# Relative biases and stores of keys and values on GpSimd's queue in a two-layer encoder step

## The chip, the cores and the metric

The kernel runs on one core of one Trainium2 chip. Its metric is device time in microseconds (us). Before the change the median is 974.71 us, of three runs of 974.71, 974.99 and 973.73 us. The engines are TensorE (PE: matmuls; PEld: its weight loads), VectorE (DVE), ScalarE (ACT), GpSimd (POOL) and SyncE (SP). SP computes nothing here: it issues DMA transfers, in the order of its own queue.

## The reference, cut to what matters

One inference step of an encoder of two layers, with 256 prompt tokens and 32 sample tokens, 1024 features, 16 heads of 64 features, all in fp32:

```
layer 0:  q,k,v of 8 heads "A" and 8 heads "B" = rmsnorm(x) @ w_in_ab
          A: s = q k^T / 8 + rel_bias[clip(pos_q - pos_k, -128, 128)]    # per head
             a query sees its own 64-token chunk and the 8 chunks before it; o = softmax(s) v
          B: stick-breaking attention (strictly causal, no softmax, no bias)
          x += [oA, oB] @ w_out_ab
layer 1:  q,k,v of 16 heads, lf = log_sigmoid(z + b_f);  c = cumsum(lf)
          s = q k^T / 8 + c_q - c_k, causal;  o = softmax(s) v;  x += o @ w_out_c
each layer then: cross-attention of 4 heads into 256 memory tokens
                 (mk, mv = rmsnorm(memory) @ w_xk, w_xv), and a SwiGLU feed-forward
returned: y, the k and v of every layer and head, lf, mk and mv of both layers
```

The sample tokens attend to cached keys and values of 128 past tokens, and to themselves. In layer 0 a prompt query thus adds to its scores, for each head, a row of the relative-distance table that starts one place later for each query; in layer 1 the bias is made from cumulative sums. Keys, values and memory keys and values are results as well as operands, so each is stored to DRAM.

## The kernel before

Features lie on the 128 partitions and the 288 tokens (256 prompt, 32 sample) along the free axis. Every fp32 product is made of three matmuls of split operands, high times high, high times low, low times high (L68 is the one line for all matmuls).

**Weights** come in units of 1024x128 (512 KB). `unit` loads one through SP (L136) into one of four buffers `st`; ACT copies it to a rounded high half `hi` (L141, five buffers), DVE subtracts to get the low half `lo` (L142, four buffers). `split_scaled` makes `hh` and `hl` (L248) of the normalized inputs in the same way, and `split` makes `kh`, `kl` and `vh`, `vl` (L314, L315) of memory keys and values; `kl` and `vl` are subtracted on POOL. POOL also adds up squares for norms (`ssq`, L213).

**Head pairs.** In both layers `pairs` runs j = 0 to 7 over pairs of heads. For each, `proj(j)` projects q, k and v (three units); `evac_kv` writes k or v to a buffer `kv` and stores it at once (L728). Then `attend(j)` starts a generator, every second pair a generator for the sample tokens, and `memory.steps` projects a few blocks of memory keys (`mk`, stored as `mkT`, L551) and values (`mv`, stored, L571) into the stream of the projections. The generators advance by a step at each `tick`, which every projection calls, so that softmax work of one pair runs beside the matmuls of the next projections.

**Softmax.** For each head the scores `sc` go to `softmax`: DVE adds the bias and takes the row maximum in one instruction (L348, one for each of the two query tiles, which have 128 and 256 key columns), ACT takes the exponential with a row sum (L350), DVE the reciprocal (L351), and DVE multiplies (L353). Then PE transposes `e` (L372 to L374). The sample's tile is `es`, transposed at L399.

**Biases in layer 0.** `rel_lines` loads the table (L737), DVE fills its left part (L738, `line`), and it is stored to DRAM (L740, `lined`). Eight copies from DRAM to DRAM (L743, one for each head) write it 128 times with rows of 385, `skew`, from which any window reads as a matrix whose rows are shifted by one. `rel_prompt` reads a head's two windows into a tile `bi` (L753: 128 columns for the first query tile, L754: 256 for the second) and POOL masks two 64x64 corners (L755, L756). Both windows are windows of the same matrix: the first tile's 128 columns are the second's columns 128 to 255. `rel_sample` makes four small loads into `bs` (L762).

**Biases in layer 1.** `gate` stores the cumulative sums (L856 `cumd`, L863 `cumsd`); `attend` loads them across partitions (L894, `ck`), and POOL subtracts and masks (L899 to L902, `bc`). For the sample, SP loads `bcs` and `cq`, and POOL subtracts and masks at L918 and L921.

**Order.** Instructions are put in order on each engine by the framework's scheduler, and each engine runs its own queue in that order; an instruction whose operand isn't ready holds up all that stand behind it on that engine. All DMA transfers of this kernel are issued by SP, so a store that waits for its data holds up the loads behind it in the same way.

## Time and profile before

| | before |
|---|---|
| median of the runs | 974.71 us (973.73 to 974.99) |
| profiled execution, own time | 973.61 us |
| its span, granted clock of TensorE | 971.8 us, 0.995 |
| PE busy | 951.7 us (98% of the span) |
| DVE, ACT, POOL busy | 588.5, 483.6, 195.9 us (61%, 50%, 20%) |
| moved by DMA | 163.59 MB, 168 GB/s in the mean |
| stores of keys and values `kv` | 32, of 144 KB each |
| stores `mkT`, `mv` | 16 and 16, of 128 KB each |
| copies `skew` | 8, of 192 KB each |
| bias loads `bi` | 8 of 128 KB and 8 of 64 KB |

How to read rows of it. A row of the timeline is: start in us from the span's beginning, duration in us, engine, source line, operation, output<-input, partitions x elements, type, and how often it runs in a row; in square brackets the idle time of that engine just ahead of it, and what ended it. SPq and POOLq are those engines' issues of DMA transfers. A row of the waits is engine and line, what it waited for, us in total, how often, and the longest. A row of the groups is line, engine, operation, output<-input, count | busy us, mean ns of one | idle time before it, and what ended most of it. A row on DMA issues gives count, KB each, and the median us from issue to landing.

### The profile page before, as it was taken

The page shows a single profiled execution, that of the slowest core. Times are in us where ns is not written, and L with a number is a line of the kernel's source. Part 1 is how long each engine was busy: PE and PEld are TensorE (multiplying, and loading weights), DVE is VectorE, ACT ScalarE, POOL GpSimd, SP SyncE. Part 2 cuts the span into 40 slices and gives each one's busy share as a digit, 9 for nine tenths or more (in the row PEclk, how much of TensorE's full clock was granted, in tenths as well). Part 3 has the DMA queues.
Part 4 walks back from the last instruction along what each step waited for, and adds up shares of the span by engine and source line. Part 5 has one row for each costly group of instructions (what it writes and reads, how often), then busy time and mean ns, then how long its engine had stood idle before and what let it go on. Part 6 is the DMA issues. An engine that isn't in the chain of part 4 may idle for free.

```text
span 971.8 us, 19089 instructions
## 1 busy us (share of the span) xinstructions
PE 951.7 (98%) x7477; PEld 919.4 (95%) x7477; DVE 588.5 (61%) x1135; ACT 483.6 (50%) x854; POOL 195.9 (20%) x293
## 2 busy tenths in 40 slices
PE   8999999999999999999999999999999999999995
PEld 7889999999999999999998999999989999999995
DVE  6687555676765555854565666657757655555452
ACT  4556868554554444443445555545546544444330
POOL 3111002210213222411004324213002222222010
PEclk9999999999999999999999999999999999999998
DMA  7775455544354444554465455545425444454431
GB/s 232 253 250 186 140 182 175 177 157 152 104 168 166 160 174 161 187 196 164 162 209 174 168 201 174 185 162 185 158 86 174 153 173 165 161 174 168 159 108 49
DMA packets 60137, 163.59 MB, mean 168 GB/s; under 512 B 8160, under 2 KB 21520, under 8 KB 60048
## 3 DMA queue, kind: packets, MB, share of 16 engines
q1 hardware_dynamic: 60048, 162.38, 49.7%
q8 instruction: 59, 0.97, 0.4%
q14 instruction: 30, 0.25, 0.1%
HBM read 152.20 MB, written 11.72 MB: 169 GB/s over the span
## 4 chain that ended last, share of the span: by engine, by line
PE 91%; DVE 3%; DMA 2%; issue 1%; ACT 1%; SPq 0%; POOL 0%; DVEq 0%; ACTq 0%; POOLq 0%
PE pj L68 51%; PE dn L68 14%; PE op L68 11%; PE mv L68 5%; DMA st<-w_ab 1%; PE xo L68 1%; PE po L68 1%; PE xs L68 1%; PE zb L68 1%; DVE lo L142 1%; PE sc L68 1%; PE nr L68 1%; PE nrm L68 1%; PE xss L68 1%; DMA x<-xT 0%
## 5 line engine op out<-in xcount | busy, mean ns | idle before, releaser
L141 ACT CAST hi<-st 128x1024 fp32r<-128x1024 f32 x260 | 272.6, 1051 | 333.3 <-issue 146.0
L68 PE MATMUL pj<-hh,hi 128*128 128x288 f32 (+1 forms) x1352 | 405.3, 300 | 0.0
L68 PE MATMUL pj<-hl,hi 128*128 128x288 f32 (+1 forms) x1352 | 398.6, 295 | 1.7 <-DVE hl L248 1.7
L68 PE MATMUL pj<-hh,lo 128*128 128x288 f32 (+1 forms) x1352 | 399.2, 295 | 0.0
L142 DVE TENSOR_TENSOR lo<-st,hi 128x1024 fp32r<-128x1024 f32 x260 | 322.8, 1242 | 125.3 <-PE dn L68 41.2
L68 PEld LDWEIGHTS pj<-hh,hi 128*128 128x128 f32 x1352 | 255.8, 189 | 6.0 <-issue 4.2
L68 PEld LDWEIGHTS pj<-hl,hi 128*128 128x128 f32 x1352 | 256.0, 189 | 3.3 <-DVE hl L248 3.2
L68 PEld LDWEIGHTS pj<-hh,lo 128*128 128x128 f32 x1352 | 255.7, 189 | 0.0
L68 PE MATMUL dn<-fh,hi 128*128 128x288 f32 x400 | 108.5, 294 | 0.0
L68 PE MATMUL dn<-fh,lo 128*128 128x288 f32 x352 | 103.3, 294 | 0.0
L68 PE MATMUL dn<-fl,hi 128*128 128x288 f32 x304 | 89.5, 294 | 0.0
L68 PE MATMUL op<-ol,hi 128*128 128x288 f32 x256 | 75.8, 297 | 0.0
L68 PE MATMUL op<-oh,hi 128*128 128x288 f32 x256 | 75.5, 297 | 0.0
L68 PE MATMUL op<-oh,lo 128*128 128x288 f32 x256 | 75.2, 294 | 0.0
L68 PEld LDWEIGHTS dn<-fh,hi 128*128 128x128 f32 x400 | 72.3, 188 | 0.0
L68 PEld LDWEIGHTS dn<-fh,lo 128*128 128x128 f32 x352 | 66.2, 188 | 0.0
L213 POOL TENSOR_TENSOR ssq<-ssq,sq 128x288 f32<-128x288 f32 (+1 forms) x37 | 35.6, 963 | 120.3 <-ACT sq L202 78.3
L68 PEld LDWEIGHTS dn<-fl,hi 128*128 128x128 f32 x304 | 57.1, 188 | 0.0
L693 POOL TENSOR_TENSOR fl<-us,fh 128x288 fp32r<-128x288 f32 x38 | 32.9, 865 | 119.3 <-ACT fh L692 119.3
L688 DVE TENSOR_TENSOR us<-pj,rstd 128x288 f32<-128x288 f32 x44 | 20.1, 457 | 59.9 <-PE pj L68 59.9
L689 POOL TENSOR_TENSOR gs<-gs,sg 128x288 f32<-128x288 f32 x44 | 38.9, 883 | 76.1 <-ACT sg L687 76.1
L68 PEld LDWEIGHTS op<-ol,hi 128*128 128x128 f32 x256 | 48.2, 188 | 0.6 <-issue 0.4
(253 smaller groups left out, 1202.7 us busy)
## 6 DMA issues: line engine op xcount, KB each, us to landing
st<-w_gate SPq DMA_DIRECT2D x44, 512.0 KB, 3.3
st<-w_up SPq DMA_DIRECT2D x44, 512.0 KB, 3.2
st<-w_down SPq DMA_DIRECT2D x44, 512.0 KB, 3.2
st<-w_c SPq DMA_DIRECT2D x25, 512.0 KB, 3.3
st<-w_ab SPq DMA_DIRECT2D x23, 512.0 KB, 4.3
st<-w_xk SPq DMA_DIRECT2D x16, 512.0 KB, 3.5
st<-w_xv SPq DMA_DIRECT2D x16, 512.0 KB, 3.4
st<-w_xq SPq DMA_DIRECT2D x16, 512.0 KB, 4.2
```

The lines of the kernel that those rows point to most:

```text
L68: T.matmul(out, lhsT, rhs, start=start, stop=stop, skip_group_check=True)
L141: S.copy(hi[:, b], st[:, b])
L142: V.tensor_tensor(lo[:, b], st[:, b], hi[:, b].bitcast(F32), ALU.subtract)
L213: eng.tensor_tensor(s[:, :self.n], self.acc[i][:, :self.n], q[:, :self.n], ALU.add)
L688: V.tensor_tensor(us, pu[:, :NT], cur.r, ALU.mult)
L689: G.tensor_tensor(gs, gs, sg, ALU.mult)
L693: G.tensor_tensor(lo, us, hi.bitcast(F32), ALU.subtract)
```

## The change

A name `SIDE` for GpSimd is added, and these transfers are issued by it and no longer by SP: the load and store of the bias line, the eight skew copies, the bias loads of layer 0 for prompt and sample, and all stores of `kv`, `mkT` and `mv`. Loads of weights, of the caches and of `ck`, `bcs` and `cq`, and the stores of `lf`, `cumd`, `cumsd` and the result, stay with SP. In `rel_prompt` one load of 256 columns takes the place of two loads of 128 and 256, and one memset of the masked corner the place of two; `softmax` gets a start column of the bias for each query tile (`at`: 128 and 0), since both tiles now read the same 256 columns. Names and arithmetic are otherwise as they were; lines after L43 move down by one or two (L348 is L350 now, L740 is L742, L743 is L745).

```diff
     V, S, G, T, DMA = nc.vector, nc.scalar, nc.gpsimd, nc.tensor, nc.sync
+    SIDE = nc.gpsimd
...
-    def softmax(s, cols, bias, out):
+    def softmax(s, cols, bias, out, at=None):
...
-                V.tensor_tensor_reduce(out=out[:, c0:c1], in0=s[:, c0:c1], in1=bias[:, c0:c1], scale=-1.0, scalar=3e38,
+                b0 = at[i] if at else c0
+                V.tensor_tensor_reduce(out=out[:, c0:c1], in0=s[:, c0:c1], in1=bias[:, b0:b0 + c1 - c0], scale=-1.0, scalar=3e38,
...
-                DMA.dma_start(a["mkT"][l, i], t[:, 0:NP])
+                SIDE.dma_start(a["mkT"][l, i], t[:, 0:NP])
...
-                        DMA.dma_start(a["mv"][l, t, :, hd * 256:hd * 256 + 256], v[:, 0:NP])
+                        SIDE.dma_start(a["mv"][l, t, :, hd * 256:hd * 256 + 256], v[:, 0:NP])
...
             V.tensor_tensor(t, p[:, :NT], cur.r, ALU.mult)
-            DMA.dma_start(dst, t)
+            SIDE.dma_start(dst, t)
...
-        DMA.dma_start(ln[:, 128:384], a["rel"][:, 0:256])
+        SIDE.dma_start(ln[:, 128:384], a["rel"][:, 0:256])
...
-        DMA.dma_start(d, ln)
+        SIDE.dma_start(d, ln)
...
-            DMA.dma_start(bass.AP(tensor=sk.tensor, ...
+            SIDE.dma_start(bass.AP(tensor=sk.tensor, ...
...
-        DMA.dma_start(t[:, 0:128], rel_rows(sk, h, 256, P, 128))
-        DMA.dma_start(t[:, 128:384], rel_rows(sk, h, 128, P, 256))
-        G.memset(t[0:64, 64:128], NEG)
-        G.memset(t[0:64, 320:384], NEG)
+        SIDE.dma_start(t[:, 0:256], rel_rows(sk, h, 128, P, 256))
+        G.memset(t[0:64, 192:256], NEG)
...
-            DMA.dma_start(t[32 * h:32 * h + 32, 0:160], rel_rows(sk, 4 * g + h, 128, NS, 160))
+            SIDE.dma_start(t[32 * h:32 * h + 32, 0:160], rel_rows(sk, 4 * g + h, 128, NS, 160))
...
-                return attend_prompt(..., o[0][j], o[1][j])
+                return attend_prompt(..., o[0][j], o[1][j], (128, 0))
```

The scheduler makes another order from it on DVE, ACT, POOL and SP; the order on PE stays. Three places are shown, numbers behind the names of tiles counting them.

**The first bias of layer 0.** SP before, from the line's store to the loads of pair 0 and the weights behind them:

```order
L740 DMA lined<-line 8x384
L136 DMA st_398<-w_ab 128x1024
L136 DMA st_462<-w_ab 128x1024
L743 DMA skew<-lined 128x384 x8
L753 DMA bi_388<-skew 128x128
L754 DMA bi_388<-skew 128x256
L753 DMA bi_393<-skew 128x128
L754 DMA bi_393<-skew 128x256
L136 DMA st_508<-w_ab 128x1024
```

POOL in the changed kernel, the same piece of work:

```order
L742 DMA lined<-line 8x384
L745 DMA skew<-lined 128x384 x8
L756 DMA bi_388<-skew 128x256
L756 DMA bi_391<-skew 128x256
L756 DMA bi_545<-skew 128x256
L756 DMA bi_548<-skew 128x256
L763 DMA bs_555<-skew 32x160
L757 MEMSET bi_388 64x64
L763 DMA bs_555<-skew 32x160
L757 MEMSET bi_391 64x64
```

Pair 0 has the tiles `bi_388` and `bi_391` (before `bi_393`), pair 1 `bi_545` and `bi_548`. POOL now issues the loads for pair 1 and one for the sample ahead of the first mask. On DVE the line's copy, which the store waits for, stands elsewhere; before:

```order
L98 CAST ntrir<-ntri 128x128
L248 SCALAR_TENSOR_TENSOR hl_197<-x_81,gain,hh_196 128x288
L738 COPY line<-line 8x128
L248 SCALAR_TENSOR_TENSOR hl_201<-x_82,gain,hh_200 128x288
```

and in the changed kernel:

```order
L249 SCALAR_TENSOR_TENSOR hl_205<-x_82,gain,hh_204 128x288
L143 TENSOR_TENSOR lo_295<-st_292,hi_294 128x1024
L125 TENSOR_SCALAR ident<-warm 128x128
L214 TENSOR_TENSOR ssq_226<-sq_222,sq_224 128x288
L128 TENSOR_TENSOR fold<-ident 128x64
L740 COPY line<-line 8x128
L143 TENSOR_TENSOR lo_348<-st_345,hi_347 128x1024
```

The copy moved behind the splits of all of the input and of a weight unit.

**The softmax of pair 1 in layer 0, on DVE.** Before, from the second head's bias (`bi_554`) to the normalized rows:

```order
L348 ISA e_629,st_630<-sc_626,bi_554 128x256
L348 ISA st_630 128x1
L351 RECIPROCAL st_618<-st_618 128x2
L348 ISA es_647,st_648<-ss_638,bs_563 128x160
L348 ISA st_648 128x1
L353 TENSOR_SCALAR e_617<-e_617,st_618 128x128
L353 TENSOR_SCALAR e_617<-e_617,st_618 128x256
L142 TENSOR_TENSOR lo_718<-st_715,hi_717 128x1024
L351 RECIPROCAL st_630<-st_630 128x2
L351 RECIPROCAL st_648<-st_648 128x1
L353 TENSOR_SCALAR e_629<-e_629,st_630 128x128
L353 TENSOR_SCALAR e_629<-e_629,st_630 128x256
```

In the changed kernel:

```order
L143 TENSOR_TENSOR lo_855<-st_852,hi_854 128x1024
L350 ISA e_609,st_610<-sc_606,bi_545 128x128
...
L350 ISA es_639,st_640<-ss_630,bs_555 128x160
L350 ISA st_640 128x1
L353 RECIPROCAL st_610<-st_610 128x2
L249 SCALAR_TENSOR_TENSOR hl_679<-mem_591,gain,hh_678 128x256
L355 TENSOR_SCALAR e_609<-e_609,st_610 128x128
L355 TENSOR_SCALAR e_609<-e_609,st_610 128x256
L353 RECIPROCAL st_622<-st_622 128x2
L353 RECIPROCAL st_640<-st_640 128x1
L355 TENSOR_SCALAR e_621<-e_621,st_622 128x128
L355 TENSOR_SCALAR e_621<-e_621,st_622 128x256
```

The split of a weight unit (`lo`) that stood between the two heads' normalizations stands ahead of the scores now; between them is one split of a memory block (`hl`).

**Layer 1.** SP before, from the stores of the cumulative sums to the first load `ck`:

```order
L863 DMA cumsd<-gw_6306 16x160
L551 DMA mkT<-mk_6316 128x256
L136 DMA st_6805<-w_c 128x1024
L551 DMA mkT<-mk_6354 128x256
L551 DMA mkT<-mk_6392 128x256
L894 DMA ck_6399<-cumd 128x512
```

SP in the changed kernel:

```order
L864 DMA cumsd<-gw_6290 16x160
L137 DMA st_6789<-w_c 128x1024
L895 DMA ck_6383<-cumd 128x512
L137 DMA st_6849<-w_xk 128x1024
```

and POOL in the changed kernel, ahead of pair 0's bias and, further on, of the first sample bias:

```order
L553 DMA mkT<-mk_6376 128x256
L316 TENSOR_TENSOR kl_6380<-mk_6376,kh_6379 128x256
L900 TENSOR_TENSOR bc_6385<-cumcol,ck_6383 128x128
L901 TENSOR_TENSOR bc_6385<-cumcol,ck_6383 128x256
L903 AFFINE_SELECT bc_6385<-bc_6385 128x128 x2
...
L730 DMA kv<-kv_6551 128x288
L553 DMA mkT<-mk_6678 128x256
L919 TENSOR_TENSOR bcs_6578<-cq_6579,bcs_6578 128x160
L922 AFFINE_SELECT bcs_6578<-bcs_6578 32x32 x4
```

The stores of memory keys no longer stand ahead of `ck` on SP; they stand ahead of biases on POOL.

More of the change, by code (lines that the diff above doesn't have):

```diff
@@ L355, in encoder_step, with attend_prompt @@
     QT = [(0, 128), (128, 384)]
-    def attend_prompt(q, k, v, vns, j, bias, oh, ol):
+    def attend_prompt(q, k, v, vns, j, bias, oh, ol, at=None):
         vn = vns[j] = v_natural(v)
@@ L366, in attend_prompt @@
             e.append(work("e"))
-            softmax(s, QT, bias[hd], e[hd])
+            softmax(s, QT, bias[hd], e[hd], at)
         yield 1
@@ L736, in rel_lines @@
         ln = cst.tile([8, 384], F32, name="line")
-        DMA.dma_start(ln[:, 128:384], a["rel"][:, 0:256])
+        SIDE.dma_start(ln[:, 128:384], a["rel"][:, 0:256])
         V.tensor_copy(ln[:, 0:128], ln[:, 128:129].to_broadcast([8, 128]))
         d = dr.tile([8, 384], F32, name="lined")
-        DMA.dma_start(d, ln)
+        SIDE.dma_start(d, ln)
         sk = dr.tile([8, 128 * 385], F32, name="skew")
         for h in range(8):
-            DMA.dma_start(bass.AP(tensor=sk.tensor, offset=sk.offset + h * 128 * 385, ap=[[385, P], [1, 384]]),
+            SIDE.dma_start(bass.AP(tensor=sk.tensor, offset=sk.offset + h * 128 * 385, ap=[[385, P], [1, 384]]),
                           bass.AP(tensor=d.tensor, offset=d.offset + 384 * h, ap=[[0, P], [1, 384]]))
@@ L781, in attend @@
             if j < 4:
-                return attend_prompt(*args, [rel_prompt(proj.line, 2 * j + i) for i in range(2)], o[0][j], o[1][j])
+                return attend_prompt(*args, [rel_prompt(proj.line, 2 * j + i) for i in range(2)], o[0][j], o[1][j], (128, 0))
             return stick_prompt(*args, o[0][j], o[1][j])
```

## The prediction

> **What bounds the kernel now.** I read the page first, then the waits of PE, then the timelines of PE, SP, DVE, POOL and ACT around each wait.
>
> ```profile
> span 971.8 us, 19089 instructions
> PE 951.7 (98%) x7477; PEld 919.4 (95%) x7477; DVE 588.5 (61%) x1135; ACT 483.6 (50%) x854; POOL 195.9 (20%) x293
> PEclk9999999999999999999999999999999999999998
> PE 91%; DVE 3%; DMA 2%; issue 1%; ACT 1%; SPq 0%; POOL 0%; DVEq 0%; ACTq 0%; POOLq 0%
> ```
>
> PE has work in 98% of the span at a full granted clock, and 91% of the chain that ended last is PE. The instructions that the change touches are on SP, POOL and DVE, so it can gain only where PE stands still for them. The waits of PE give that as one row:
>
> ```profile
> PE tp L372 <- DVE e L353: 4.7, 6, 1.9
> ```
>
> Six times, 4.7 us in all, PE waits for the normalized softmax rows (e, written by DVE) before it transposes them. Here are those with an idle time beside them, in the timeline of PE:
>
> ```profile
> 32.53 0.30 PE L372 MATMUL tp<-ident,e 128*128 128x128 f32 x1 [0.54 <-DVE e L353]
> 33.41 0.30 PE L372 MATMUL tp<-ident,e 128*128 128x128 f32 x1 [0.27 <-DVE e L353]
> ...
> 48.20 0.33 PE L372 MATMUL tp<-ident,e 128*128 128x128 f32 x1 [1.09 <-DVE e L353]
> ...
> 62.43 0.30 PE L372 MATMUL tp<-ident,e 128*128 128x128 f32 x1 [0.70 <-DVE e L353]
> ...
> 63.27 0.33 PE L372 MATMUL tp<-ident,e 128*128 128x128 f32 x1 [0.23 <-DVE e L353]
> ...
> 522.86 0.30 PE L372 MATMUL tp<-ident,e 128*128 128x128 f32 x1 [1.87 <-DVE e L353]
> ```
>
> These are four places: pair 0 of layer 0 (0.54 + 0.27 = 0.81 us), pair 1 (1.09), pair 2 (0.70 + 0.23 = 0.93), pair 0 of layer 1 (1.87). Their sum is 4.70 us: the most the change can win here, 0.5% of the span. Elsewhere PE does not stand still: from 90 to 250 us, where SP also issues stores, it is busy for 159.95 of 160 (the columns of these windows are length, busy time of PE, weight loads, DVE, ACT and POOL, granted clock, share of the DMA engines, GB/s).
>
> ```profile
> 12.00:31.00 19.00, 19.00 (x130) 18.46 (x131) 12.46 (x32) 6.27 (x12) 1.03 (x7) 1.00 0.83 249
> 90.00:250.00 160.00, 159.95 (x1309) 152.61 (x1307) 100.15 (x179) 100.03 (x177) 21.72 (x22) 1.00 0.49 161
> ```
>
> So the 98 issues that leave SP are worth nothing by themselves: about 0.4 us each, on a queue that mostly waits.
>
> **The change part by part.** The unknown is G, the time for which one DMA issue holds POOL; no row has POOL issuing one. On SP an issue took between 0.33 and 0.63 us: eight skew copies 5.05 us. On POOL, work over 128 partitions took 0.96 us in the mean (ssq) and up to 1.48 us (kl).
>
> ```profile
> 12.49 0.30 SPq L740 DMA_DIRECT2D lined<-line  x1
> ...
> 13.88 5.05 SPq L743 DMA_DIRECT2D skew<-lined  x8
> ```
>
> ```profile
> L213 POOL TENSOR_TENSOR ssq<-ssq,sq 128x288 f32<-128x288 f32 (+1 forms) x37 | 35.6, 963 | 120.3 <-ACT sq L202 78.3
> ```
>
> ```profile
> 92.76 1.48 POOL L315 TENSOR_TENSOR kl<-mk,kh 128x256 fp32r<-128x256 f32 x1 [21.56 <-ACT kh L314]
> ...
> 25.32 0.15 POOL L755 MEMSET bi<- 64x64 f32 x1 [14.27 <-DMA bi<-skew]
> ```
>
> I take G = 0.96 us, POOL's own mean for a pass over 128 partitions, because the work moves to POOL, and keep 0.33 (SP's shortest) and 1.48 as ends. Of the Trainium skill, "DMA: Bandwidth & Descriptors", section "Latency and other measured facts", gives about 1 us to the first byte for a DMA from GpSimd and 0.6 for one from SP; by that ratio the skew's 0.63 us would become about 1.05, an estimate from that page, and the sum below would be 1.35 us less good: 972.4 in place of 971.0.
>
> *First bias of layer 0.* Before, POOL writes its mask at 25.32 and DVE adds the bias at 30.55; SP had issued the copies from 13.88.
>
> ```profile
> 12.25 0.21 DVE L738 COPY line<-line 8x128 f32<-8x128 f32 x1
> ...
> 14.94 0.21 DVE L127 TENSOR_TENSOR fold<-ident 128x64 f32<-128x64 f32 x1
> ...
> 30.55 0.29 DVE L348 CUSTOM_DVE_ANT_0 e<-sc,bi 128x128 f32<-128x128 f32 x1
> ...
> 32.98 0.55 DVE L353 TENSOR_SCALAR e<-e,st 128x128 f32<-128x128 f32 x2
> ```
>
> In the new order DVE's copy of the line stands behind fold, so it starts near 14.95 instead of 12.25 (fold ends its slot at 15.08, and the old copy's 0.13 us ahead of it is gone). POOL issues the store of the line 0.24 us later, at 15.2 (as SP did, 12.25 to 12.49). That takes G, and landing 1.09 us more (13.88 - 12.49 - 0.30): 16.3 + G. Then POOL issues in order 8 skews, 4 biases and 1 sample bias, writes the first mask, issues another sample bias, writes the second mask: the second head's bias is usable at T = 16.3 + 15 G. The first copy's landing is no later bound: with 7.1 us it lands at 24.4, before the eighth issue ends at 24.9, and the bias's own 4.0 us end before its mask.
>
> ```profile
> skew<-lined SPq DMA_DIRECT2D x8, 192.0 KB, 7.1
> ...
> bi<-skew SPq DMA_DIRECT2D x8, 128.0 KB, 4.0
> ```
>
> PE comes to its transposes at 31.99 (32.53 - 0.54), and to the second head's 0.61 later (32.53 to 33.41 less 0.27), at 32.6. From adding the bias to transposing it took 1.98 us (30.55 to 32.53), so PE does not wait if T is at most 30.6. With G = 0.96, T = 30.7: a wait of 0.1 in place of 0.81, a gain of 0.7. Above that each 0.1 us of G costs 1.5 us. What queues behind on DVE are the next weights' low halves and K and V, and PE waits for all of them.
>
> *Pairs 1 and 2.* DVE's order put a split of weights (lo, 1.22 us) between the scores and the normalization, waiting for weights that SP had issued late:
>
> ```profile
> 46.53 1.22 DVE L142 TENSOR_TENSOR lo<-st,hi 128x1024 fp32r<-128x1024 f32 x1
> ...
> 60.66 1.22 DVE L142 TENSOR_TENSOR lo<-st,hi 128x1024 fp32r<-128x1024 f32 x1
> ```
>
> In the new order those splits stand ahead of the scores, at a time when DVE waits for PE anyhow; only a 0.47 us piece is left between. I count 1.09 and 0.83 of the 0.93 as gained. Pair 1's biases are issued by 29.7 us (16.3 + 14 x 0.96), far ahead of its normalization near 46.
>
> *Layer 1, pair 0.* DVE waited for POOL's bias, POOL for the load ck, and SP issued that behind two stores of keys:
>
> ```profile
> 512.21 2.28 SPq L551 DMA_DIRECT2D mkT<-mk  x2
> 514.59 0.38 SPq L894 DMA_DIRECT2D ck<-cumd  x1
> ...
> ck<-cumd SPq DMA_DIRECT2D x8, 256.0 KB, 3.6
> ...
> 513.29 0.42 DVE L550 TENSOR_TENSOR mk<-pj,memrow 128x256 f32<-128x256 f32 x1 [1.22 <-PE pj L68]
> ...
> 514.61 0.84 POOL L315 TENSOR_TENSOR kl<-mk,kh 128x256 fp32r<-128x256 f32 x1 [1.21 <-ACT kh L314]
> 518.95 0.40 POOL L899 TENSOR_TENSOR bc<-cumcol,ck 128x128 f32<-128x128 f32 x1 [3.51 <-DMA ck<-cumd]
> ```
>
> ```profile
> 516.84 1.22 DVE L142 TENSOR_TENSOR lo<-st,hi 128x1024 fp32r<-128x1024 f32 x1
> 520.21 0.29 DVE L348 CUSTOM_DVE_ANT_0 e<-sc,bc 128x128 f32<-128x128 f32 x1 [2.15 <-POOL bc L902]
> ...
> 517.81 1.28 ACT L350 ACT_TABLE_LOAD   x1
> ```
>
> Without the stores ck goes out at 512.2 and lands at 515.8. POOL has by then issued the third key store (keys ready at 513.71, plus 0.96) and done kl (0.84): 515.5. So the bias starts at 515.8 instead of 518.95, and the next bound is DVE's lo, ending at 518.06, then ACT's table, at 519.09. The rest of the first head's softmax (1.98 less 0.3 for adding the bias) ends at 520.8, before PE comes at 520.99 (522.86 - 1.87); the second head's ends 0.88 later (32.53 to 33.41 in layer 0), at 521.65, where PE is ready at about 521.5. Of 1.87 us I count 1.7 as gained.
>
> *The new wait in layer 1.* In pair 1 POOL must now issue a key store, which waits for mk, ahead of the sample's bias:
>
> ```profile
> 531.25 0.42 DVE L550 TENSOR_TENSOR mk<-pj,memrow 128x256 f32<-128x256 f32 x1 [1.77 <-PE pj L68]
> ...
> 531.98 1.84 POOL L921 TENSOR_SCALAR_AFFINE_SELECT bcs<-bcs 32x32 f32<-32x32 f32 x4
> ...
> 534.01 0.31 DVE L348 CUSTOM_DVE_ANT_0 es<-ss,bcs 128x160 f32<-128x160 f32 x1
> ...
> 536.71 0.27 PE L399 MATMUL ts<-ident,es 128*128 128x128 f32 x1
> ```
>
> With all 1.7 earlier: mk at 529.97, its store until 530.93, bias and masks 2.4: 533.3, where DVE wants it at 532.3. Behind it on DVE stand both heads' normalizations. Between es and its transposes lie 2.70 us (534.01 to 536.71), of which the softmax needs about 2.3 (1.98 and a third head's 0.3), so PE has 0.4 of the 1.0 to spare: 0.6 lost. With G at 0.33 nothing, at 1.48 about 1.1.
>
> *Costs that stay covered.* The other key and value stores add about 60 issues to a POOL that is busy 20% of the time; even 90 x 0.96 = 86 us leave it under 30%. Half the bias loads and 8 x 64 KB vanish: at 249 GB/s some 2 us of transfers while PE is busy for 19.00 of 19; nothing by itself. The loads of x come first in both.
>
> The sum: 0.7 + 1.09 + 0.83 + 1.7 - 0.6 = 3.7 us gained. The profiled execution took 973.61 us (1.8 around its span) and would take 969.9; the median of the runs is 1.1 above it: 974.71 - 3.7 = **971.0**. With G = 0.33 the gain is 0.81 + 1.09 + 0.83 + 1.7 = 4.4 (970.3); with G = 1.48 the first bias is usable at 38.5, PE waits 7.9 us, and the sum is 7.9 - 0.81 - 1.09 - 0.83 - 1.7 + 1.1 = 4.6 slower (979.3).
>
> **The rivals.** *The first bias comes too late.* The mechanism is T = 16.3 + 15 G: 13 issues in a row on POOL before a mask can be written. The wait is 15 G - 14.3. At G = 1.21 it eats the gain, from 1.34 the kernel is slower by 0.2%; 1.4 gives a wait of 6.7 and a time of 977.6. For it: POOL's rows are longer than SP's throughout. Against it: the bias had 5.2 us of slack (25.32 to 30.55).
>
> *The waits only move.* DMA engines are 83% busy from 12 to 31 us. If weights and skew copies now in flight together delay each other, DVE's splits still come late, and the 1.92 us of pairs 1 and 2 stay: 974.71 - 3.7 + 1.92 = 972.9. For it: that share; against it: 0.5 MB less is moved, and SP's loads start sooner. The Trainium skill, same page, section "Issuing engines are not separate DMA queues", says that all issuers share the same 16 engines and that spreading issues saves only sequencer time; it would have this result. The trace shows more than sequencer time: a load held behind stores that waited for DVE.
>
> *POOL holds up others.* If stores in POOL's queue delay biases in all four odd pairs of layer 1 as in pair 1, that costs 3 x 0.6 more: 972.8. For it: such a store stands ahead of each sample's bias; against it: in the later pairs that store waits for keys that DVE has written well before.
>
> **How the numbers follow.** Forecast 0.54, late bias 0.21, moved waits 0.17, POOL holds up others 0.08. A difference under about 0.2% (1.95 us) cannot be told from none. Faster: the forecast, and a little of the moved waits: 0.56. Slower: the upper part of the late bias: 0.16. Same: the rest, 0.28. The forecast's own range is 970 to 972.5; with the late bias up to G = 1.4 and 1 us for the runs' own spread I give 969 to 978.5.
>
> **What would show it.** Right: POOL's issues near 1 us; the first mask by 30 us; the waits of PE for e in pairs 1 and 2 gone; ck issued near 512 and the layer 1 wait under 0.5. Wrong: POOL still issuing skews at 28 us, DVE waiting for a mask, PE idle over 2 us near 32; or a wait of DVE for the sample bias in layer 1.

## The result: 0.6% slower

The changed kernel takes 980.58 us in the median (978.80 to 981.16, four runs), the kernel before 974.22 us (973.60 to 974.99, four runs): a ratio of 1.0061, 95% interval [1.0049, 1.0073]. The prediction was 971.0 us with a range of 969 to 978.5, and a chance of 0.16 for slower. It was wrong in its sign. The profiled execution took 980.78 us.

The page of the changed kernel, the parts that answer to those shown of before:

```profile
span 979.1 us, 19107 instructions
PE 951.5 (97%) x7477; PEld 920.2 (94%) x7477; DVE 591.1 (60%) x1135; ACT 483.0 (49%) x854; POOL 247.0 (25%) x375
PEclk8899999999999999999999999999999999999997
```

PE is as busy as before, in a span that is 7.3 us longer, so PE stands still for longer; and its clock is below full in the first two slices. The waits of PE, the row that was 4.7 us in six waits:

```profile
PE tp L374 <- DVE e L355: 7.8, 3, 6.8
```

One wait of 6.8 us has taken the place of several of 0.2 to 1.9. The timeline of PE in the changed kernel, at the transposes whose rows of before the prediction shows (32.53, 48.20, 63.27 and 522.86), and at matmuls behind the first:

```profile
38.36 0.45 PE L374 MATMUL tp<-ident,e 128*128 128x128 f32 x1 [6.78 <-DVE e L355]
...
43.03 0.44 PE L69 MATMUL pj<-hl,hi 128*128 128x288 f32 x1
43.27 0.38 PE L69 MATMUL pj<-hh,lo 128*128 128x288 f32 x1
43.48 0.30 PE L69 MATMUL pj<-hh,hi 128*128 128x288 f32 x1
43.62 0.29 PE L69 MATMUL pj<-hl,hi 128*128 128x288 f32 x1
...
54.22 0.27 PE L374 MATMUL tp<-ident,e 128*128 128x128 f32 x1
...
67.73 0.28 PE L374 MATMUL tp<-ident,e 128*128 128x128 f32 x1
68.50 0.33 PE L375 MATMUL tp<-ident,e 128*128 128x128 f32 x1 [0.48 <-DVE e L355]
...
527.83 0.30 PE L374 MATMUL tp<-ident,e 128*128 128x128 f32 x1 [0.83 <-DVE e L355]
```

Since PE's order stays, one instruction's two starts give how late the changed kernel is at that place. It is 5.8 us late at the first transposes (38.36 against 32.53). Behind them matmuls start 0.24 us apart until 43.3 and 0.14 after that, as if PE's clock were halved for 5 us: the same matmul that starts at 35.74 before starts at 43.27 here, 7.5 us late. The waits of pairs 1 and 2 are gone but for 0.48 us, which brings it down to 5.0 (68.50 against 63.53). A new wait in the cross-attention of layer 0 makes it 5.4; from there it grows slowly to 6.0 in stretches where PE waits no longer than before. The shorter wait in layer 1 gives 1.1 back, a second new wait in cross-attention takes 0.4 again, and by the end it is 4.2 us late, as the issue of the result's stores shows, of before and of the changed kernel:

```profile
965.97 2.85 SPq L955 DMA_DIRECT2D yT<-yo  x4
```

```profile
970.15 2.85 SPq L956 DMA_DIRECT2D yT<-yo  x4
```

But the span is 7.3 us longer, so 3.1 us are lost behind the last work of all. They stand in the rows of the kernel's closing instructions (engine and operation, count: shortest/median/longest in ns, first and last start), before and after:

```profile
L1019 POOLq DRAIN  x3: 34/78/1482, 965.3 to 971.5; - x3
```

```profile
L1020 POOLq DRAIN  x3: 46/102/8851, 969.4 to 978.8; - x3
L1020 SPq DRAIN  x3: 7/7/7, 975.3 to 978.5; - x3
```

POOL's closing drain has grown from 1.48 to 8.85 us. It starts beside the last multiplications at 969.4 and ends at 978.3, while SP, which waits for the stores' landing, begins its own first drain at 975.3.

The two new waits, of 0.30 us each, make PE 0.37 us later each time. They are for the normalized rows `xe` of cross-attention, which DVE writes beside POOL's subtraction `vl`. In layer 0, before and changed:

```profile
248.82 1.10 DVE L353 TENSOR_SCALAR xe<-xe,st 128x256 f32<-128x256 f32 x2
248.96 0.80 POOL L315 TENSOR_TENSOR vl<-mv,vh 128x256 fp32r<-128x256 f32 x1 [0.31 <-DMA mv<-mv]
```

```profile
253.86 1.54 DVE L355 TENSOR_SCALAR xe<-xe,st 128x256 f32<-128x256 f32 x2
253.93 0.56 POOL L573 DMA_DIRECT2D mv<-mv  x1
254.51 0.74 POOL L316 TENSOR_TENSOR vl<-mv,vh 128x256 fp32r<-128x256 f32 x1
```

In both, DVE's second multiplication ends 0.15 us behind POOL's subtraction (249.92 and 249.76, 255.40 and 255.25). In the changed kernel the issue of the store `mv` stands ahead of that subtraction on POOL, and both come later. The same two waits stand in the traces of e2, e9, e10 and e12 below, where POOL issues these stores, and in no other; why DVE ends with POOL there, no run shows.

So four losses, 5.8 + 1.7 + 0.7 + 3.1 us, stand against 2.6 gained in pairs 1 and 2, 1.1 in layer 1, and a drift of 0.4 (0.7 lost up to layer 1, 1.1 gained behind it) that was not explained: 7.2 of the 7.3 us.

How the first bias came late is read from the chain of POOL's issues, with DVE's copy ahead of it, of the changed kernel; the first load's row of before follows, which the prediction did not show:

```profile
14.87 0.21 DVE L740 COPY line<-line 8x128 f32<-8x128 f32 x1
...
15.38 0.59 POOL L742 DMA_DIRECT2D lined<-line  x1 [4.41 <-DVE line L740]
19.85 4.19 POOL L745 DMA_DIRECT2D skew<-lined  x8 [3.87 <-DMA lined<-line]
26.59 0.57 POOL L756 DMA_DIRECT2D bi<-skew  x1 [2.55 <-DMA skew<-lined]
...
36.18 0.15 POOL L757 MEMSET bi<- 64x64 f32 x1 [3.85 <-DMA bi<-skew]
```

```profile
20.98 0.34 SPq L753 DMA_DIRECT2D bi<-skew  x1
```

| link of the chain | before | changed |
|---|---|---|
| copy of the line starts | 12.25 | 14.87 |
| its start to the store's issue | 0.24 | 0.51 |
| store to first skew copy | 1.39 | 4.47 |
| first skew copy to first bias load | 7.10 | 6.74 |
| first bias load to first mask | 4.34 | 9.59 |
| first mask | 25.32 | 36.18 |

Two transfers are slow, the line's store by 3.1 us and the first load by 5.3. The issues themselves are not: eight skew copies hold POOL for 4.19 us, 0.52 each, less than SP's 0.63. In the meantime SP runs ahead: from the line's store to the first bias load (15.38 to 26.59) it issues four weight units, two caches and a block of memory, 3 MB; before (12.49 to 20.98) it issued two weight units, 1 MB.

### The profile page after: what moved, and what is told of

Read it like the earlier page. It is cut to its first block, busy times and chain, and to the rows that moved or that the text cites. A ratio compares the mean times of both kernels' runs of the same rounds, so it can differ in the third digit from the quotient of the medians.

```text
span 979.1 us, 19107 instructions
## 1 busy us (share of the span) xinstructions
PE 951.5 (97%) x7477; PEld 920.2 (94%) x7477; DVE 591.1 (60%) x1135; ACT 483.0 (49%) x854; POOL 247.0 (25%) x375
## 4 chain that ended last, share of the span: by engine, by line
PE 91%; DVE 3%; DMA 3%; issue 1%; ACT 1%; POOL 1%; SPq 0%; DVEq 0%; POOLq 0%; ACTq 0%
PE pj L69 52%; PE dn L69 14%; PE op L69 10%; PE mv L69 5%; PE po L69 1%; PE xo L69 1%; DMA bi<-skew 1%; PE zb L69 1%; PE sc L69 1%; PE xs L69 1%; DMA skew<-lined 1%; PE xss L69 1%; PE nr L69 1%; DMA x<-xT 0%; PE xt L614 0%
## 5 line engine op out<-in xcount | busy, mean ns | idle before, releaser
L695 POOL TENSOR_TENSOR fl<-us,fh 128x288 fp32r<-128x288 f32 x38 | 32.8, 863 | 119.4 <-ACT fh L694 119.4
```

Source lines behind the costliest of these rows:

```text
L695: G.tensor_tensor(lo, us, hi.bitcast(F32), ALU.subtract)
```

## The experiments

Two questions came out of the traces. The first: what makes those transfers late? Theory P: a transfer issued by POOL is slow by itself. Theory Q: with the chain on a queue of its own, SP's queue no longer stands behind it and runs ahead with weights, caches and memory, and both share the DMA engines, so that what is needed first arrives late. Theory R: the chain merely starts late, behind DVE's splits. The second: what sets the length of the drain?

All ratios are to the kernel before, timed on the same chip.

| kernel | issues by POOL | ratio [95% interval] | median us | first mask | PE's waits for e in pair 0 | drain us |
|---|---|---|---|---|---|---|
| before | 0 | | 974.2 to 974.6 | 25.3 | 0.8 | 1.48 |
| changed | 90 | 1.0061 [1.0049, 1.0073] | 980.6 | 36.2 | 6.8 | 8.85 |
| e1: 256 columns, all on SP | 0 | 0.9968 [0.9957, 0.9979] | 971.0 | 26.0 | 1.5 | 1.48 |
| e2: e1, stores on POOL | 64 | 0.9981 [0.9973, 0.9990] | 972.5 | 26.2 | 1.5 | 6.73 |
| e3: e1, line, skew, biases on POOL | 26 | 1.0018 [1.0008, 1.0028] | 976.8 | 35.1 | 5.2 | 3.62 |
| e4: before, one load on POOL | 1 | 0.9999 [0.9990, 1.0007] | 974.0 | 25.2 | 0.8 | 1.57 |
| e5: e1, line and skew on POOL | 10 | 1.0030 [1.0018, 1.0042] | 977.2 | 31.4 | 6.7 | 2.31 |
| e7: e1, bias loads on POOL | 16 | 1.0011 [1.0002, 1.0020] | 975.7 | 27.9 | 3.7 | 2.81 |
| e10: changed, line filled by POOL | 90 | 1.0052 [1.0037, 1.0067] | 979.7 | 32.8 | 3.3 | 8.84 |
| e11: e1, 1.5 MB needless loads on POOL | 6 | 1.0023 [1.0013, 1.0033] | 976.2 | 29.4 | 3.8 | 1.99 |
| e6: e1, line and skew on ACT | 0 | 1.0065 [1.0048, 1.0082] | 981.1 | 15.8 | 0 | 1.48 |
| e9: changed, POOL's last work on DVE | 90 | 1.0037 [1.0024, 1.0049] | 977.8 | 35.9 | 5.8 | 8.27 |
| e12: changed, PE kept busy in the wait | 90 | 1.0048 [1.0035, 1.0062] | 978.6 | 36.4 | 0.3 | 8.85 |
| e8: e1, three key stores on POOL | 3 | 0.9950 [0.9937, 0.9964] | 968.7 | 26.0 | 0.5 | 1.75 |

### The columns alone, the stores alone, the biases alone

e1 keeps of the change only `rel_prompt` and `softmax`:

```diff
-    SIDE = nc.gpsimd
+    SIDE = nc.sync
```

> The changed kernel with every transfer back on SP; of the change only the 256 bias columns in one load and the one mask are left. Theory A (three losses: the first bias late by POOL's slow path, 6.2 us; PE at half clock after that wait, 1.7; POOL's closing drain, 3.0; against gains of 1.7, 0.9 and 1.1 in pairs 1 and 2 of layer 0 and pair 0 of layer 1): all three losses are gone, no DRAIN of POOL above 2 us. Theory C (the gains come from the new order that the scheduler makes, not from a freed SP): about 974.2 - 1.7 - 0.9 = 971.6. Its rival D (the gains need the stores off SP's queue): 974.2 within 0.7, and PE still waits about 1 us in pair 1 and 2 us in pair 0 of layer 1.

e2 and e3 give POOL one half of the issues each (`DMA` is SP). Two places of e2's edit are shown; e3 leaves these with POOL and gives the stores of `kv`, `mkT` and `mv` to SP:

```diff
 e2
-        SIDE.dma_start(d, ln)
+        DMA.dma_start(d, ln)
...
-        SIDE.dma_start(t[:, 0:256], rel_rows(sk, h, 128, P, 256))
+        DMA.dma_start(t[:, 0:256], rel_rows(sk, h, 128, P, 256))
```

> Only the stores of kv, mkT and mv are issued by POOL (64 issues); line, skew and bias transfers are back on SP, with 256 columns. Theory A: the first bias is on time and PE stays at full clock, the wait in layer 1 falls below 1 us, and the closing drain of POOL still ends about 3 us after the last output has landed: 974.2 + 3.0 - 1.1 - (0 to 2.6) = 973.5 to 976.1. Theory B (all that was lost comes from the first bias; the drain hides behind the output's landing): 970.5 to 973.

> Only line, skew and bias transfers are issued by POOL (all in the first 60 us); the stores are back on SP. Theory A: the first mask near 36 us, PE waits some 6 us and then runs 4 to 5 us at half clock, layer 1 waits 2 us again, and the drain of POOL is there although its last DMA was issued 900 us before: 980.6 + 1.1 = about 981.7. If the drain only stands for transfers still under way at the end, it is gone: about 978.7. Theory B: 977 to 979 as well, told apart by the drain's record (above 7 us under A, below 2 under B).

The columns alone are faster by 0.32%, and need no freed queue for it: theory C, not D, for pairs 1 and 2. The timeline of PE in e1 at the second heads' waits of these pairs and in layer 1:

```profile
46.77 0.33 PE L374 MATMUL tp<-ident,e 128*128 128x128 f32 x1 [0.36 <-DVE e L355]
...
60.93 0.33 PE L375 MATMUL tp<-ident,e 128*128 128x128 f32 x1 [0.35 <-DVE e L355]
...
520.26 0.30 PE L374 MATMUL tp<-ident,e 128*128 128x128 f32 x1 [1.63 <-DVE e L355]
```

1.09 and 0.93 us have become 0.36 and 0.35. In layer 1 the wait is still there (1.63 against 1.87): there it is SP's stores, as D has it. The drain is 1.48 us, as before. Some 1.1 us of e1's lead grows slowly through stages in which PE waits no longer in one kernel than in the other; that part was not explained.

The stores on POOL (e2) cost 0.13% against e1, 1.3 us; the two intervals overlap a little. Layer 1 is cured (its first transposes wait for nothing, against 1.63), and the drain, 6.73 us, ends 1.0 us behind the last landing that SP waits for; PE also waits 0.9 us for the sample's softmax in pair 1 of layer 0 and twice 0.30 in cross-attention. The expectation's 3.0 us for the drain were too many, and the time lies below theory A's range: the drain is shorter than the changed kernel's. The biases on POOL (e3) cost 0.50% against e1, 4.9 us: the chain is nearly as late as in the changed kernel (first mask 35.1, PE waits 5.24), but the drain, 3.62 us, hides behind the landing of the result, so the time is below all that was expected. The two halves add up to 6.2 us, the whole costs 9.1 (1.0061 less 0.9968): 2.0 of the rest are the drain, which both halves lengthen and only the whole brings far into the open (3.0 against 1.0), and 1.0 the first transposes, 38.36 against 37.33.

### The price of the drain

```diff
-        DMA.dma_start(bf, a["b_f"])
+        G.dma_start(bf, a["b_f"])
```

> The kernel before with a single transfer on POOL: the load of 16 gate biases (64 bytes), needed 470 us later. No other instruction moves. Theory A, drain as a fixed price of the first DMA on POOL: about 974.2 + 3.0 = 977.2, with a POOL DRAIN of 7 to 9 us at the end. A price that grows with the number of DMAs on POOL (93 in the changed kernel, 3.0 us): 974.2, DRAIN below 2 us. Theory B: 974.2.

(The change moves 90 issues, not the 93 that the expectation counts.) No fixed price: with one issue the drain is 1.57 us, and the time is that of before. The rows of e4, e2 and e3, beside the two above:

```profile
L1019 POOLq DRAIN  x3: 46/93/1570, 965.0 to 971.3; - x3
```

```profile
L1020 POOLq DRAIN  x3: 45/102/6727, 962.7 to 970.2; - x3
```

```profile
L1020 POOLq DRAIN  x3: 46/102/3619, 967.1 to 973.5; - x3
```

Over all kernels but e9 it is a straight line: 1.48 us and 0.082 for each issue of POOL in the whole program (1: 1.57; 3: 1.75; 6: 1.99; 10: 2.31; 16: 2.81; 26: 3.62; 64: 6.73; 90: 8.85), though in e3 the last of them was issued 900 us earlier. It counts issues, not bytes: 64 stores of 8.9 MB and 26 biases of 2.8 MB lie on one line. The drain ends 1.0 us late with 6.73 us and 3.0 late with 8.85, so some 5.8 us of it, 52 issues, are free behind the result's own landing (an estimate from these two).

e9 lets POOL's work end earlier, and leaves its issues:

```diff
-            eng, s = (G, r) if m0 < 6 and i == 1 else (V, p)
+            eng, s = V, p
```

> The changed kernel, but POOL's last two multiplications (of the result) are done by DVE, so that POOL's last work ends near 957 in place of 971. If the closing drain is POOL's own time after its last work (8.85 us with 90 issues), it runs from 957 to 966 beside PE's last matmuls and ends before the output lands: 3.0 us less, 0.8 more for DVE: 978.4. If it waits for transfers still under way, or for SP's stores, it ends where it did: 981.4.

```profile
L1020 POOLq DRAIN  x3: 46/102/8269, 956.5 to 976.4; - x3
```

Still 8.27 us long, but begun at 956.5 and over at 964.8, 11 us before the result has landed: 977.8 us, 2.8 less than the changed kernel. Behind SP's first closing drain 0.8 us are left of the span, as before the change; in the changed kernel it was 3.8. POOL's last DMA was issued at 726. So the drain is POOL's own time after its last instruction, and waits neither for SP's stores nor for a transfer of its own that is still under way.

### What makes the first bias late

e5 and e7 split the chain between the queues; both leave all stores to SP, and one place of each is shown:

```diff
 e5
-        SIDE.dma_start(t[:, 0:256], rel_rows(sk, h, 128, P, 256))
+        DMA.dma_start(t[:, 0:256], rel_rows(sk, h, 128, P, 256))
 e7
-        SIDE.dma_start(d, ln)
+        DMA.dma_start(d, ln)
```

> Of the transfers only the line's load, the line's store and the eight skew copies are issued by POOL; bias loads and all stores by SP, 256 columns. Stages of the chain in the runs so far (store of the line issued, first skew issued, first bias load issued, first mask): on SP 12.0, 13.4, 19.8, 26.0; on POOL 15.4, 19.9, 26.6 to 27.0, 35.1 to 36.2. Theory P (each link issued by POOL is slow by itself): store 15.4, skew 19.9, first load near 27, and from there SP's 4.3 to 6.2 us: first mask near 32, PE waits 2 to 3 us, time 971 + 2.5 + 1 = 974 to 975. Theory Q (what costs is that transfers in POOL's queue share the engines with weights and cache loads of SP): here SP's loads stand behind the bias loads, so the copies run alone: skew to first load no more than 6.5 us, first mask by 30, PE waits less than 1.5 us, 971 to 973.

> The counterpart: line, skew and all stores on SP, only the bias loads of layer 0 (16 issues) on POOL, 256 columns. Theory P: chain as on SP up to the skew (13.4), the first load issued near 20, and then POOL's 8 to 9.6 us to the first mask: 28 to 29.6. DVE adds the bias at 30.3 anyway: no wait of PE beyond the 1.2 us of the columns-only kernel, time 971 within 0.7. Theory Q: the loads share the engines with the weights that SP issues right behind the skew: the same, or later (30 and more), PE waits 1 to 3 us, 971 to 974. Under both the drain of POOL is 1.48 + 16 x 0.082 = 2.8 us and hidden.

Both theories missed e5's time. Its first mask came at 31.4, near P's 32, and only 4.3 us after the first skew copy the first load went out, quicker than SP ever was (6.3 to 7.1). But PE waited 6.7 us all the same, until 38.3. The timeline of ACT in e5 tells for what:

```profile
31.91 0.40 ACT L352 ACTIVATE e<-e,st 128x128 f32<-128x128 f32 x1 [3.96 <-DVE st L350]
...
35.48 1.04 ACT L142 CAST hi<-st 128x1024 fp32r<-128x1024 f32 x1 [3.07 <-DMA st<-w_ab]
36.43 0.50 ACT L352 ACTIVATE e<-e,st 128x256 f32<-128x256 f32 x1
```

A weight unit that was late stood ahead of the other exponentials in ACT's order. SP had issued it only at 31.41, behind bias loads that waited for the skew copies, and it landed in 4.0 us: here the order of SP's queue made it late, which neither theory had. In e7, where the mask was in time (27.9, nearly as P said), a unit is late again, but for another reason: it is issued at 24.5 and takes 7.1 us to land, ACT waits 3.11 us for it, and PE 2.65 and 1.02 us for the softmax behind it. Its time, 975.7, lies above both theories' too. So what is late need not be what POOL issued.

e10 starts the chain earlier:

```diff
-        V.tensor_copy(ln[:, 0:128], ln[:, 128:129].to_broadcast([8, 128]))
+        G.tensor_copy(ln[:, 0:128], ln[:, 128:129].to_broadcast([8, 128]))
```

> The changed kernel, but the 8x128 fill of the line is done by POOL itself right after its sums of squares, in place of DVE behind its splits: the chain starts at about 11.1 in place of 14.9. Theory R (the start is what was late): all links 3.8 us earlier, first mask near 32.4, PE waits 3 us in place of 6.8: 980.6 - 3.8 = 976.8, and 1 less if the spell at half clock gets shorter. Theory Q: the copies now meet the weights of the start (the engines 90% busy from 12 to 31 us) and gain less than 2 us: 978.5 to 980.5. The drain stays at 8.9 us.

```profile
11.54 0.59 POOL L742 DMA_DIRECT2D lined<-line  x1 [0.30 <-POOL line L740]
15.65 4.18 POOL L745 DMA_DIRECT2D skew<-lined  x8 [3.52 <-DMA lined<-line]
22.77 0.57 POOL L756 DMA_DIRECT2D bi<-skew  x1 [2.94 <-DMA skew<-lined]
...
32.78 0.15 POOL L757 MEMSET bi<- 64x64 f32 x1 [3.65 <-DMA bi<-skew]
```

3.8 us earlier at the start gave 3.4 at the mask, and 3.7 us less of that wait; but PE now waits 1.5 us for values elsewhere, and the time is 979.7, 0.9 less, with intervals that overlap. Theory R, 976.8, falls: the links stay slow wherever they lie in this stretch.

e6 puts line and skew on ACT's queue.

```diff
-            SIDE.dma_start(bass.AP(tensor=sk.tensor, ...
+            S.dma_start(bass.AP(tensor=sk.tensor, ...
```

> As the kernel with the chain on POOL, but the line and the eight skew copies are issued by ScalarE's queue, which POOL's software has no part in; ScalarE's own work (hh, hi) stands behind the issues that wait for the line. Theory P (POOL's issue is what is slow): store of the line to first skew about 1.4 us, skew to first load about 7. Theory Q (sharing the engines with SP's loads): skew to first load 9 us and more, though no software is in it. The time itself is not told apart by it (ScalarE is held up at the start by some 1 to 3 us: 971 to 976).

This does not decide between P and Q. The line's store took 3.2 us to the first skew copy (3.24 to 6.42; P had 1.4), the copy 6.6 to the first load (P had 7, Q 9 and more). But the chain ran 10 us earlier, where it meets other transfers, and ACT was held up for longer than expected, so that PE waited 4.20 us for a weight unit and 4.79 for the norm's squares, and the time missed its range:

```profile
14.55 1.97 ACTq L745 DMA_DIRECT2D skew<-lined  x3
16.56 1.04 ACT L142 CAST hi<-st 128x1024 fp32r<-128x1024 f32 x1 [5.05 <-issue]
```

e11 is the test of Q by itself. Nothing that anyone waits for is issued by POOL; it only loads 1.5 MB that nobody reads while the chain runs on SP:

```diff
+    for i in range(6):
+        t = work("extra")
+        G.tensor_copy(t[:, 0:1], cur.norm.acc[0][:, 0:1])
+        G.dma_start(t, a["cmk"][1, i % 4])
     memories = [Memory(0), Memory(1)]
```

> The columns-only kernel (chain, loads and stores all on SP, in its order) with six needless loads of 256 KB issued by POOL from about 12 us on, while the line's store and the skew copies are under way; no other instruction moves. 1.5 MB is 6 us at the 250 GB/s of this stage. Theory Q (transfers of two queues share the engines, so the ones that are needed first come later): first skew to first bias load more than 6.3 us, first mask after 28 in place of 26.0 or a weight unit late, PE waits 3 us and more near 32 in place of 1.2: 973 to 977. Theory P (only what POOL itself issues is slow): 971 within 0.7, since POOL issues nothing that anyone waits for. Drain 1.48 + 6 x 0.082 = 2.0 us, hidden.

```profile
16.35 3.37 POOL L942 DMA_DIRECT2D extra<-cmk  x6
29.42 0.41 POOL L757 MEMSET bi<- 64x64 f32 x2 [9.71 <-DMA bi<-skew]
```

```profile
31.01 1.05 ACT L142 CAST hi<-st 128x1024 fp32r<-128x1024 f32 x1 [6.64 <-DMA st<-w_ab]
```

The six loads went out from 16.35 on, not from 12: behind the line's store, which they therefore do not test, and beside the skew copies. The mask comes 3.4 us later than in e1, a weight unit is late by more (ACT waits 6.64 us for it), PE waits 3.79, and the time is 976.2 against 971.0: theory Q's numbers. The stretches of e1, e11 and the changed kernel (length, busy time of PE, weight loads, DVE, ACT, POOL, clock, share of the DMA engines, GB/s):

```profile
26.00:32.00 6.00, 4.99 (x39) 4.21 (x37) 3.07 (x13) 2.90 (x10) 0.58 (x4) 1.00 0.83 273
```

```profile
26.00:32.00 6.00, 5.79 (x45) 5.01 (x43) 0.00 (x0) 0.99 (x2) 0.59 (x4) 1.00 1.01 378
```

```profile
26.00:32.00 6.00, 5.58 (x43) 4.80 (x41) 1.59 (x2) 2.51 (x4) 2.37 (x5) 1.00 1.03 324
```

With the second queue the engines are full, and in the changed kernel they are as full while its first bias is on its way. That sharing is enough to make this stage lose 5 us is shown by e11. In the changed kernel SP's own loads of that time are as slow as the bias, even one of 64 bytes (rows of DMA issues from 24 to 27 us: count, KB each, us to landing):

```profile
st<-w_ab SPq DMA_DIRECT2D x1, 512.0 KB, 10.6
...
bi<-skew POOLq DMA_DIRECT2D x1, 128.0 KB, 9.5
...
bf<-b_f SPq DMA_DIRECT2D x1, 0.1 KB, 12.2
```

So the bias is not slow because POOL issued it. Against P also stand POOL's stores where the engines are not full, which land no later than SP's (rows of DMA issues, before and after):

```profile
kv<-kv SPq DMA_DIRECT2D x32, 144.0 KB, 3.2
```

```profile
kv<-kv POOLq DMA_DIRECT2D x32, 144.0 KB, 2.6
```

For the line's store, 3.1 us of the loss, no run separates the two. It lands after 4.2 us at 19.6, just behind a unit and two caches that SP issued from 14.3 to 15.1 (17.9 to 19.5), with the engines 91% busy from 16 to 20 us; before, they were 18% busy from 12 to 14. That fits Q, but a share of POOL's own is not excluded.

By the section "Issuing engines are not separate DMA queues" of "DMA: Bandwidth & Descriptors" in the Trainium skill, all issuers' transfers run on the same 16 engines and interleave; the runs agree (e11), and add what it costs, 5.2 us there, when transfers that are not needed yet come from a second queue.

### The half clock

e12 puts needless matmuls on PE where it waited:

```diff
             t = att("tp")
+            for i in range(fill if hd == 0 else 0):
+                T.matmul(t[:, 0:P], identb, identb, start=True, stop=True, skip_group_check=True)
             T.transpose(t[:, 0:128], e[hd][:, 0:128], ident)
```

> The changed kernel with 110 needless 128x128 matmuls on the identity just ahead of pair 0's transposes, where PE stood idle for 6.8 us; they write the tile that the transposes then overwrite. If the idle time is what brought the 5 us at half clock, PE keeps full clock there (0.13 us from matmul to matmul behind the transposes in place of 0.24) and 1.7 us come back: 980.6 - 1.7 = 978.9. If the half clock has another cause (load on the chip, DMA), it stays: 980.6; and more if the added matmuls last beyond the wait.

The stretch behind the transposes, of the changed kernel and of e12:

```profile
38.00:44.00 6.00, 5.64 (x25) 5.25 (x26) 2.72 (x7) 2.36 (x6) 3.38 (x10) 0.55 0.59 183
```

```profile
38.00:44.00 6.00, 5.64 (x45) 4.58 (x42) 3.51 (x9) 3.33 (x8) 3.39 (x10) 1.00 0.57 182
```

The transposes start at the same time (38.46 against 38.36), the granted clock is 1.00 in place of 0.55, 45 matmuls take the place of 25, and by the end of the spell PE is 1.6 us further: the idle time did bring the half clock. Of these 1.6 us 1.0 are given back in pair 1, where PE waits 0.75 us for the sample's softmax instead, and 0.2 in pair 2. The time, 978.6, is as expected, but its interval overlaps with the changed kernel's, and the two traces' spans are alike (979.2 and 979.1), so the price in time stays open between 0.4 and 1.7 us. The Trainium skill, "TensorE: Matmul & The Clock Gate", part 1 on the clock gate, gives an idle window of about 3.4 us for halving the clock and as long a busy one for restoring it; the runs agree in kind, but not on the length, since shorter waits did it too. Told by matmuls that start 0.24 us apart in the timelines, every wait of PE of 2.65 us and more in this stage (changed, e3, e5, e7, e9, e10, e11) was followed by 3 to 6 us at half clock. Of the waits of 1.4 to 1.9 us at layer 1's first transposes, those of e4, e5 and e6 (1.81, 1.71, 1.56) were followed by some 3 us of it, and those of before, e1, e3, e7 and e11 by none.

### A version that beats both

e8 leaves all on SP, with the 256 columns, but for three stores:

```diff
-                SIDE.dma_start(a["mkT"][l, i], t[:, 0:NP])
+                (G if l == 1 and i < 3 else DMA).dma_start(a["mkT"][l, i], t[:, 0:NP])
```

> The columns-only kernel (everything on SP) with three issues moved: the first three stores of memory keys in layer 1, which stand ahead of the load ck on SP, are issued by POOL. Nothing else moves on any engine. Theory D (a store that waits for its data holds ck back): ck is issued about 0.8 us earlier, the wait of PE in pair 0 of layer 1 falls from 1.6 us to under 0.5, the drain of POOL is 1.48 + 3 x 0.082 = 1.7 us and hidden: ratio to before 0.9968 - 0.0015 = 0.9953, about 970. Rival: DVE's split and the table load bound that softmax anyway, or the landing of ck takes what was gained: 0.9968.

```profile
509.83 0.39 SPq L895 DMA_DIRECT2D ck<-cumd  x1
```

```profile
518.65 0.30 PE L374 MATMUL tp<-ident,e 128*128 128x128 f32 x1
```

The load ck goes out right behind its cumulative sums, in e1 (at 511.87) behind two stores; PE's wait of 1.63 us is gone, and its transposes start 1.6 us earlier than in e1 (518.65 against 520.26). 968.7 us, a ratio of 0.9950 [0.9937, 0.9964] to before: three of the 90 moved issues carry the gain that moving stores has here. (Its interval and e1's overlap by a hair; the traces' 1.6 us between them say the same as the medians' 2.3.)

## Why the prediction was wrong

**The bound.** Right in the main: PE bounds the kernel, and the 98 issues that left SP were worth nothing by themselves. But 4.7 us were not the most that could be won: the trace of e8 is 5.3 us shorter than that of before (966.5 against 971.8) with 1.4 us of such waits left, since part of its lead, as of e1's, grows elsewhere, unexplained.

**G and the first bias.** Here lies the step that failed: the landing times. G itself was too dear. It was taken as 0.96 us from passes over 128 partitions, which is another kind of work; POOL's issues in this chain took 0.52 to 0.59. (The 0.33 to 0.63 us given for SP's issues were too narrow as well: SP's issues of before took 0.30 to 1.37.) By the prediction's own formula, T = 16.3 + 15 G, that gives 24.6 and no wait, and one of its signs of failure, POOL still issuing skews at 28 us, did not show (the eighth ended at 24.0). Yet the first mask came at 36.2, and the other signs showed: DVE waited for it, and PE stood idle for 6.8 us. What failed are the terms that were taken from before as they stood: 1.09 us for the line's store to land (3.9 here) and 4.0 for the bias itself (9.5 here). The first copy's 7.1 held (6.5), but as the issues were short it did bind: POOL stood idle for 2.55 us until it landed, where the prediction had "no later bound". These times had been measured where one queue carried everything, in the order in which it was needed; on two queues they are prices under load, and the sum of issues was not what bounds. The late start of DVE's copy was read rightly from the new order (14.95, measured 14.87).

**The late bias as a rival.** It had the right place and wait (977.6 at a wait of 6.7 us; the wait was 6.8), by luck: its reason was the time of issues, and by its formula the measured issues give no wait. It also left out what an idle PE costs behind the wait: 1.7 us at half clock.

**The waits only move.** This rival had the mechanism, transfers of weights and copies that delay each other, and the profile line that speaks for it, 83% share from 12 to 31 us. But it was priced as a gain not made (1.92 us), on pairs 1 and 2, where the gain came; the collision was one stage earlier and cost some 6 us.

**Pairs 1 and 2.** Right: 1.92 us were counted, some 2.6 came (1.5 of it as waits in the rows shown; the rest was not traced). The reason was right for the changed kernel (the split of weights stands ahead of the scores there), but e1 gets most of it with the split still between the two heads, so that order is not the only way to it.

**Layer 1, pair 0.** Right in kind: ck behind two stores of keys was the cause, as e8 shows with three issues. 1.7 us were counted and 1.1 came in the changed kernel, since ck landed after 4.8 us in place of 3.6; in e2 and e8 nearly all came.

**The new wait of the sample's bias.** Right in place, too dear: DVE waits 0.39 us for it, and PE not at all, against 0.6 counted.

**Costs that stay covered.** Right for most of the stores, but not for all: POOL's issue of `mv` ahead of its subtraction cost PE 0.37 us in each layer's cross-attention, where the prediction had nothing.

**What was not thought of.** The closing drain: 3.1 us. Nothing in the trace of before could show its price for each issue; but its row was there, on POOL, and no term stood for what lies behind the last instruction.

The sum, with measured terms: in place of 0.7 gained in pair 0, 5.8 and then 1.7 lost; 2.6 and 1.1 gained; 0 for the sample's bias; 0.7 lost in cross-attention and 3.1 at the end; 0.4 gained by the unexplained drift.

## What to carry to other kernels

An order of transfers on one queue is also a priority. Before a chain that is needed early goes to a second queue, look at the share of the DMA engines in that stretch and ask what the freed queue will fetch in the meantime: where they are busy, landing times of the old trace no longer hold. Move only the issues that hold something back (here three of the 90 that were moved), and look for what each issuing engine must do after its last instruction.

## What the runs showed of the hardware

- POOL's closing drain takes 1.48 us and 0.082 for each DMA it issued in the program (0 to 90 issues, in all kernels that ran but e9, where 90 took 8.27), whatever their size and however long ago; it runs from POOL's last instruction on, and can be hidden by ending POOL's work earlier (e9).
- An issue held POOL for 0.50 to 0.73 us, in the median 0.56 in the changed kernel; SP's took 0.33 in the median before, but up to 1.37.
- Stretches in which PE never waits differ by up to 0.4% between two executions, in both directions. The same 982 matmuls behind cross-attention took 130.44 us before and 131.00 in the changed kernel in layer 0, and 130.19 and 129.68 in layer 1. The changed kernel loses 0.56 us in the one and gains 0.51 in the other: single drifts of this size in the comparison of two traces mean nothing.
- PE fell to half clock after waits as short as 1.56 us (e6), and not after each of that size: 2.65 us and more did it in all seven executions that had such a wait in pair 0, 1.4 to 1.9 us in three of eight.
- DVE's two multiplications of `xe` took 0.62 us in most heads, 1.10 beside POOL's subtraction before the change, and 1.54 where an issue stood ahead of that subtraction.
